# Spacing the activation and split-weight tiles of a two-layer decoder trunk by 64 bytes more than their length

## The chip, the core and the metric

The kernel runs as one program on one core of a Trainium2 chip. The metric is the device time of one execution in microseconds (us). The core has a matrix engine (TensorE: "PE" for its matmuls and "PEld" for its weight loads in the profile), VectorE ("DVE"), ScalarE ("ACT"), GpSimd ("POOL") and a queue engine ("SP") that issues most DMAs. Its working memory has 128 partitions. A tile takes the same range of bytes in each partition that it uses, and "address" below is the first byte of that range within a partition.

## The reference

The reference computes a decoder trunk of two layers on x of 512 tokens by 1024 features, in float32. Cut to the skeleton:

```
hn = rmsnorm(h, norm_mix[layer])
mix = even_mixer(...)  or  odd_mixer(...)      # input projection, attention, output projection
h = h + mix
h = h + square(relu(rmsnorm(h, norm_mlp[layer]) @ w1)) @ w2      # hidden width 4096
out = rmsnorm(h, norm_final)
```

Layer 0 mixes by differential and forgetting attention, layer 1 by a sparse attention that keeps the 128 best keys of each query. What matters here are the products of activations (1024 x 512 tokens) with weight matrices: the input and output projections of both layers and the two MLPs.

## The kernel before

**Split products.** Each of these products is made from two parts per operand. A float32 value is cast to float32r, which gives the high part, and the rest (value minus high part) is the low part. `split` (L178) makes both: ScalarE casts (L179), VectorE or, for some weights, GpSimd subtracts (L180). `gemm_steps` (L351) then adds three matmuls into one PSUM tile for each of the 8 blocks k of 128 input features: high weights times high activations (L355), high weights times low activations (L356), low weights times high activations (L357). Each of them loads 128 x 128 weights and streams 512 token columns of activations past them. The weight load of the next matmul runs while the current matmul streams, so TensorE then reads two things from memory at once: the activations of this matmul and the weights of the next.

**Weights.** `emit_split` (L291) loads 256 columns of a weight matrix into a `raw` tile and splits 128 columns at a time into a `whl` tile of shape (128, 2, 8, 128): 8192 bytes per partition, high parts in the first 4096 bytes and low parts in the last 4096, 512 bytes for each k. There are 3 `whl` buffers, used in turn. `wnext` keeps one tile split ahead of the one in use.

**Activations.** The normed or mixed activations lie in 16 `gh` tiles (8 high, 8 low; `norm` L214, `first_norm` L241, `o_split` L675) of 2048 bytes each. In the MLP (`mlp`, L681) the hidden layer is made in two halves of 2048 features: `proj` (L396) multiplies `gh` with w1, and `fin` (L687) turns each result into a high and a low tile with the tag `act`, 32 tiles of 2048 bytes; `out_gemm` (L629) multiplies the 16 pairs of `act` with w2. The last 128 features of the last product are made in two pieces of 256 columns (`last_pair`, L646).

**Places in memory.** Tiles of a pool lie one behind another, so the address of one moves all that follow it. In the built program `whl` lies at 42560, 50752 and 58944, `gh` at 67136 + 2048 n, and `act` at 134784 + 2048 n in layer 0 and 151168 + 2048 n in layer 1. Modulo 256 this is 64 for all of `whl`, 64 for all of `gh`, and 128 for all of `act`. The slices within a tile begin at multiples of 512 bytes from its start, so every slice has its tile's remainder. The attention's tiles have one remainder per layer: `qk`, `P`, `PT` and `vs` all have 128 in layer 0 and 0 in layer 1. The constant `onesr` has 192, `scr` 64.

**Order.** The order of the work on each engine is the order in which the program is written; `weave` (L364) interleaves the threads of the attention stages by their counts of steps. In the MLPs and output projections TensorE runs the matmuls of `gemm_steps` one after another with nothing between them.

Of the kernel before, what the change touches and what calls it, by code (L numbers as in the profile page):

```python
# [11 lines left out]
F32R = mybir.dt.float32r  # L12
# [5 lines left out]
P = 128  # L18
S = 512
D = 1024  # L20
NT = S // P
KB = D // P
# [16 lines left out]
WHL_BUFS = 3  # L39
# [38 lines left out]
def trunk(ctx, tc, x, norm_mix, w_in_even, b_forget, lambda_q1, lambda_k1, lambda_q2, lambda_k2,  # L78
# [4 lines left out]
    wts = ctx.enter_context(tc.tile_pool(name="wts", bufs=2))  # L83
# [5 lines left out]
    def blk(tag, bufs, shape=(P, S), dt=F32, pool=None):  # L89
        tile_n[0] += 1  # L90
        return (pool or big).tile(list(shape), dt, name=f"{tag}_{tile_n[0]}", tag=tag, bufs=bufs)

    def ptile(tag, bufs):
        tile_n[0] += 1
        return ps.tile([P, S], F32, name=f"{tag}_{tile_n[0]}", tag=tag, bufs=bufs)
# [3 lines left out]
    pT = lambda: ptile("pT", B_PT)  # L99
    pO = lambda: ptile("pO", B_PO)  # L100
    scr = lambda: blk("scr", 5)
    small = lambda n, dt=F32: blk(f"sm{n}", 6, (P, n), dt, sm)


    xv = x.rearrange("o (t p) d -> p (o t) d", p=P)
    load = tc.tile_pool(name="load", bufs=1, reuse_waits="tile")
    lpool = load.__enter__()
    xt = [blk("xw", 4, (P, NT, WC), pool=lpool) for c in range(D // WC)]
    vecs = lpool.tile([16, P], F32, name="vecs")

# [67 lines left out]
    def split(dst_hi, dst_lo, src, eng=None):  # L178
        nc.scalar.copy(dst_hi, src)  # L179
        (eng or nc.vector).tensor_sub(dst_lo, src, dst_hi.bitcast(F32))  # L180
# [33 lines left out]
    def norm(gcol, rope_tab):  # L214
        gh = []
        acc = scr()
        for j in range(KB):
            hi = blk("gh", 16, dt=F32R)
            lo = blk("gh", 16, dt=F32R)
            g = cols[:, gcol + j:gcol + j + 1]  # L220
            nc.scalar.activation(hi, h[j], AF.Copy, scale=g)
            nc.vector.scalar_tensor_tensor(lo, h[j], g, hi.bitcast(F32), op0=OP.mult, op1=OP.subtract)
            gh.append((hi, lo))
            if j == 0:
                nc.scalar.activation(acc, h[j], AF.Square)
            else:
                sq = scr()
                nc.scalar.activation(sq, h[j], AF.Square)
                nc.vector.tensor_add(acc, acc, sq)
        r_tables(rsqrt_cols(acc, 1.0 / D), rope_tab)  # L230
        return gh
# [9 lines left out]
    def first_norm(w, c0):  # L241

        load_x(1)
        emit_split()
        load_x(2)
        load_x(3)
# [44 lines left out]
    def emit_split():  # L291
        w, r0, c0, c, n, wd, lo = plan.pop(0)
        if c == 0:
            raw = blk("raw", RAW_BUFS, (P, KB, WC), F32, wts)
            nc.sync.dma_start(raw[:, :, :wd], w[r0:r0 + D, c0:c0 + wd].rearrange("(k p) c -> p k c", p=P))
            raws[0] = raw
        t = blk("whl", WHL_BUFS, (P, 2, KB, P), F32R, wts)
        split(t[:, 0, :, :n], t[:, 0, :, n:2 * n] if n == 8 else t[:, 1, :, :n], raws[0][:, :, c:c + n], lo)
        ready.append((t, w, r0, c0 + c))

    def wnext(w, r0, c):
        while plan and len(ready) <= AHEAD:
            emit_split()
        t, w_, r_, c_ = ready.pop(0)
        assert (r_, c_) == (r0, c) and w_.tensor.name == w.tensor.name
        return t
# [89 lines left out]
    def proj(w, gh, c0, fin):  # L396
        r = []
        for c in range(0, WC, P):
            wt = wnext(w, 0, c0 + c)
            p = pg()  # L400
            gemm(p, wt, gh)
            fin(p, r.append)
        return r
# [225 lines left out]
    def out_gemm(w, r0, acts, done=None, early=()):  # L629
        nr = len(acts) // KB  # L630
        for s in range(D // WC):
            if done is not None and s == D // WC - 1:
                last_pair(w, r0, acts, s, done)
                return
            pp = early if early and s == 0 else [pg() for c in range(0, WC, P)]
            for r in range(nr):
                for i, p in enumerate(pp):
                    if pp is not early:
                        gemm(p, wnext(w, r0 + r * D, s * WC + i * P), acts[r * KB:(r + 1) * KB], start=(r == 0), stop=(r == nr - 1))
                    if r == nr - 1:  # L640
                        j = s * WC // P + i
                        nc.vector.tensor_add(h[j], h[j], p)  # L642
                        if done is not None:
                            done(j)
# [36 lines left out]
    def mlp(ap, layer, done=None):  # L681
        gh = norm(16 + KB * layer, False)
        half = 2 * D
        w1, w2 = w_mlp_in[layer], w_mlp_out[layer]
        for f0 in range(0, D_FF, half):
            acts = []
            def fin(p, put):  # L687
                t = blk("t", 3, pool=ap)
                nc.vector.scalar_tensor_tensor(t, p, 0.0, r_b, op0=OP.max, op1=OP.mult)  # L689
                hi = blk("act", 32, dt=F32R, pool=ap)  # L690
                lo = blk("act", 32, dt=F32R, pool=ap)
                nc.scalar.activation(hi, t, AF.Square)
                sq = blk("t", 3, pool=ap)
                nc.scalar.activation(sq, t, AF.Square)
                nc.vector.tensor_sub(lo, sq, hi.bitcast(F32))
                put((hi, lo))

            for s in range(half // WC):
                acts += proj(w1, gh, f0 + s * WC, fin)
            out_gemm(w2, f0, acts, done if f0 + half == D_FF else None)  # L700
# [316 lines left out]
```

## Time and profile before

| | |
|---|---|
| median of 3 runs | 1266.65 us (1266.27 to 1266.7) |
| the profiled execution | 1266.42 us, of which 1264.6 us from the first to the last instruction |
| granted TensorE clock | 0.999 |
| matmuls / weight loads | 5882 / 5882 |
| busy: PE / PEld / DVE / ACT / POOL | 99% / 81% / 57% / 44% / 8% |
| HBM read / written | 111.18 MB / 6.29 MB |

Stages by the trace's windows: first norm and first products up to about 60 us, attention of layer 0 to about 230, output projection and MLP of layer 0 to about 620, input products and attention of layer 1 to about 870, output projection and MLP of layer 1 to the end.

A row that groups instructions has the line, the engine, the operation, the tile written and the tiles read (buffer numbers left out), the shapes and the count; behind the first bar the busy time in us and the mean duration of one in ns; behind the second bar the idle time ahead of them, and what ended it. Since matmuls overlap, the duration of one is longer than the distance from its start to the start of the next, and its end is modelled. The distance between starts is called pitch here.

### The profile page before, as it was taken

To read this page: it belongs to the slowest core of one execution; us is meant where nothing else is said; L and a number is where in the kernel's file an instruction comes from. 1 tells how busy PE (TensorE), PEld (TensorE's weight loads), DVE (VectorE), ACT (ScalarE), POOL (GpSimd) and SP (SyncE) were. 2 spreads that over 40 slices of the span, in tenths; PEclk is the share of its full clock that TensorE was granted. 3 is DMA by queue.
4 is the path that set the end of the run, shared out by engine and by line. 5 is a ranking of instruction groups with operands and counts; after the bars stand their busy time and mean duration, and the time that the engine had idled before them with its cause. 6 is when DMAs were issued, how large, how long until landed. Compare 5 with 4: busy or idle time off the path is not lost.

```text
span 1264.6 us, 15517 instructions
## 1 busy us (share of the span) xinstructions
PE 1246.9 (99%) x5882; PEld 1029.2 (81%) x5882; DVE 721.7 (57%) x1386; ACT 558.2 (44%) x1013; POOL 100.0 (8%) x75
## 2 busy tenths in 40 slices
PE   8999999999999999999999999999999999999998
PEld 6778888888888888888788888887888888888887
DVE  7887669664432244434499987787644322444232
ACT  5456667443321133323353578885533211333231
POOL 2000000000000000000114533230000000000000
PEclk9999999999999999999999999999999999999999
DMA  8646342333322233233335344524333223332321
GB/s 240 152 122 165 98 139 79 114 100 100 100 100 98 79 93 98 100 117 109 133 100 153 95 124 117 154 76 133 100 100 98 87 85 97 100 100 100 100 67 67
DMA packets 145898, 138.92 MB, mean 110 GB/s; under 512 B 7480, under 2 KB 130528, under 8 KB 145824
## 3 DMA queue, kind: packets, MB, share of 16 engines
q1 hardware_dynamic: 144848, 136.66, 36.4%
q0 software_dynamic: 528, 0.67, 0.3%
q8 instruction: 46, 0.75, 0.2%
q10 hardware_dynamic: 448, 0.60, 0.2%
q14 instruction: 28, 0.23, 0.1%
HBM read 111.18 MB, written 6.29 MB: 93 GB/s over the span
## 4 chain that ended last, share of the span: by engine, by line
PE 87%; DVE 5%; ACT 3%; DMA 2%; issue 1%; SPq 1%; POOL 0%; POOLq 0%; DVEq 0%; ACTq 0%
PE pg L355 26%; PE pg L357 26%; PE pg L356 26%; DMA raw<-in_w_in_even_dram 2%; PE pT L514 2%; PE pS L480 1%; PE pS L481 1%; ACT P L488 1%; PE pO L533 1%; PE pO L532 1%; DVE whl L180 1%; ACT whl L179 1%; PE pT L449 1%; DVE P L486 1%; DVE PT L180 1%
## 5 line engine op out<-in xcount | busy, mean ns | idle before, releaser
L179 ACT CAST whl<-raw 128x1024 fp32r<-128x1024 f32 (+1 forms) x198 | 206.5, 1044 | 538.6 <-PE pg L357 486.2
L355 PE MATMUL pg<-gh,whl 128*128 128x512 f32 x1064 | 421.3, 397 | 3.9 <-ACT whl L179 3.8
L357 PE MATMUL pg<-gh,whl 128*128 128x512 f32 x1064 | 416.0, 392 | 1.4 <-DVE whl L180 1.3
L356 PE MATMUL pg<-gh,whl 128*128 128x512 f32 x1064 | 415.2, 391 | 0.0
L180 DVE TENSOR_TENSOR whl<-raw,whl 128x1024 fp32r<-128x1024 f32 x174 | 211.4, 1216 | 180.7 <-ACT whl L179 180.4
L357 PEld LDWEIGHTS pg<-gh,whl 128*128 128x128 f32 x1064 | 199.4, 187 | 44.0 <-DVE whl L180 2.5
L355 PEld LDWEIGHTS pg<-gh,whl 128*128 128x128 f32 x1064 | 199.5, 188 | 42.4 <-ACT whl L179 4.9
L356 PEld LDWEIGHTS pg<-gh,whl 128*128 128x128 f32 x1064 | 199.8, 188 | 38.6
L355 PE MATMUL pg<-act,whl 128*128 128x512 f32 (+1 forms) x528 | 204.5, 387 | 0.0
L357 PE MATMUL pg<-act,whl 128*128 128x512 f32 (+1 forms) x528 | 203.4, 385 | 0.0
L356 PE MATMUL pg<-act,whl 128*128 128x512 f32 (+1 forms) x528 | 201.4, 382 | 0.0
L689 DVE SCALAR_TENSOR_TENSOR t<-pg,r_b 128x512 f32<-128x512 f32 x64 | 44.3, 692 | 156.2 <-PE pg L357 153.7
L357 PEld LDWEIGHTS pg<-act,whl 128*128 128x128 f32 x528 | 99.1, 188 | 21.8
L356 PEld LDWEIGHTS pg<-act,whl 128*128 128x128 f32 x528 | 99.1, 188 | 20.9
L355 PEld LDWEIGHTS pg<-act,whl 128*128 128x128 f32 x528 | 99.3, 188 | 18.6
L488 ACT ACTIVATE P<-P,sm 128x128 f32<-128x128 f32 (+3 forms) x128 | 71.7, 561 | 50.2 <-DVE sm L486 49.8
L642 DVE TENSOR_TENSOR h<-h,pg 128x512 f32<-128x512 f32 x46 | 31.4, 687 | 108.3 <-PE pg L357 108.3
L180 POOL TENSOR_TENSOR whl<-raw,whl 128x1024 fp32r<-128x1024 f32 x24 | 57.7, 2406 | 122.2 <-ACT whl L179 100.7
L190 POOL TENSOR_TENSOR sm<-sm,nhalf 128x4 f32<-128x4 f32 (+1 forms) x9 | 10.4, 1153 | 648.1 <-DVE sm L188 648.1
L180 DVE TENSOR_TENSOR PT<-pT,PT 128x384 fp32r<-128x384 f32 (+1 forms) x84 | 49.7, 597 | 19.2 <-ACT PT L179 18.6
L179 ACT CAST PT<-pT 128x384 fp32r<-128x384 f32 (+1 forms) x84 | 42.4, 510 | 13.9 <-PE pT L514 13.3
L514 PE MATMUL pT<-ident,P 128*128 128x128 f32 x280 | 46.5, 275 | 1.7 <-ACT P L501 0.8
(230 smaller groups left out, 1180.6 us busy)
## 6 DMA issues: line engine op xcount, KB each, us to landing
raw<-in_w_mlp_in_dram SPq DMA_DIRECT2D x32, 1024.0 KB, 5.4
raw<-in_w_mlp_out_dram SPq DMA_DIRECT2D x32, 1024.0 KB, 4.8
qk<-qk SPq DMA_DIRECT2D x156, 128.0 KB, 2.3
raw<-in_w_in_even_dram SPq DMA_DIRECT2D x24, 512.0 KB, 4.7
raw<-in_w_in_odd_dram SPq DMA_DIRECT2D x16, 512.0 KB, 4.0
raw<-in_w_in_odd_dram SPq DMA_DIRECT2D x6, 1024.0 KB, 5.1
raw<-in_w_out_even_dram SPq DMA_DIRECT2D x4, 1024.0 KB, 5.2
h<-hd SPq DMA_DIRECT2D x16, 256.0 KB, 5.7
```

The source lines that it names most:

```text
L179: nc.scalar.copy(dst_hi, src)
L180: (eng or nc.vector).tensor_sub(dst_lo, src, dst_hi.bitcast(F32))
L355: nc.tensor.matmul(pout, wt[:, 0, k, :n], a, start=start and k == 0, stop=False)
L356: nc.tensor.matmul(pout, wt[:, 0, k, :n], b, start=False, stop=False)
L357: last_mm[0] = nc.tensor.matmul(pout, wt[:, 1, k, :n], a, start=False, stop=stop and k == KB - 1)
L449: nc.tensor.transpose(q[:, t * P:(t + 1) * P], y[:, t * P:(t + 1) * P], ident)
L480: nc.tensor.matmul(sp[m][:, c], qb[m][:, q], kb[0][m][:, :w], start=True, stop=False)
L481: nc.tensor.matmul(sp[m][:, c], qb[m][:, q], kb[1][m][:, :w], start=False, stop=(rows is None))
L488: nc.scalar.activation(o, o, AF.Exp, bias=st[m][:, t:t + 1], scale=-1.0, accum_out=st[m][:, 4 + t:5 + t])
L514: nc.tensor.transpose(p[:, o - o0 + (t - kt) * P:o - o0 + (t - kt + 1) * P], pt[:, OFF[t] + kt * P:OFF[t] + (kt + 1) * P], ident)
L642: nc.vector.tensor_add(h[j], h[j], p)
L689: nc.vector.scalar_tensor_tensor(t, p, 0.0, r_b, op0=OP.max, op1=OP.mult)
```

## The change

A helper `odd_blk` takes a tile 16 elements (64 bytes) longer than asked and hands out its first n columns. The `whl` tiles and both `act` tiles are made with it:

```diff
+    def odd_blk(tag, bufs, n, dt, pool):
+
+        return blk(tag, bufs, (P, n + 16), dt, pool)[:, :n]
...
-        t = blk("whl", WHL_BUFS, (P, 2, KB, P), F32R, wts)
+        t = odd_blk("whl", WHL_BUFS, 2 * KB * P, F32R, wts).rearrange("p (a k c) -> p a k c", a=2, k=KB)
...
-                hi = blk("act", 32, dt=F32R, pool=ap)
-                lo = blk("act", 32, dt=F32R, pool=ap)
+                hi = odd_blk("act", 32, S, F32R, ap)
+                lo = odd_blk("act", 32, S, F32R, ap)
```

The buffers are then 8256 and 2112 bytes apart. In the built program `whl` lies at 42560, 50816 and 59072, that is 64, 128 and 192 modulo 256. All that follows `whl` moves up by 192 bytes: `gh` to 67328 + 2048 n, remainder 0 for all 16 tiles; `act` to 134976 + 2112 n and 151360 + 2112 n, remainders 64, 128, 192, 0 in turn, so that a high tile and its low tile differ by 64. `qk`, `P`, `PT` and `vs` move together, to 64 in layer 0 and 192 in layer 1; `scr` to 0; `onesr`, `ident` and `raw` stay.

The instructions and their order are the same on every engine, and every shape that an instruction reads or writes. One wait is new, on ScalarE ahead of the first write into `act` in layer 0. Before, the rows there (line, operation, tiles with their numbers, and the semaphores waited for) are:

```order
L179 CAST whl_2810<-raw_2772 128x1024 [waits PE_49,Activation_49]
L179 CAST scr_2728<-scr_2726 128x512 [waits DVE_49,Activation_49]
L236 COPY r_b<-pT_2732 128x512 [waits PE_49]
L692 ACTIVATE act_2766<-t_2764 128x512 [waits DVE_49]
L694 ACTIVATE t_2769<-t_2764 128x512
```

Now, with lines 4 further down in the file, they are:

```order
L183 CAST whl_2810<-raw_2772 128x1024 [waits PE_49,Activation_49]
L183 CAST scr_2728<-scr_2726 128x512 [waits DVE_49,Activation_49]
L240 COPY r_b<-pT_2732 128x512 [waits PE_49]
L696 ACTIVATE act_2766<-t_2764 128x512 [waits DMAHW2_49,DVE_49]
L698 ACTIVATE t_2769<-t_2764 128x512
```

Nothing has moved; the write of the first `act` tile also waits for a DMA (DMAHW2), because the longer tile reaches 64 bytes into the place of a second `qk` tile of the attention before.

## The prediction

> **What bounds the kernel now.** I read the page first, for the engine that sets the time: its span, its busy times and the chain of work that ended last.
>
> ```profile
> span 1264.6 us, 15517 instructions
> PE 1246.9 (99%) x5882; PEld 1029.2 (81%) x5882; DVE 721.7 (57%) x1386; ACT 558.2 (44%) x1013; POOL 100.0 (8%) x75
> PE pg L355 26%; PE pg L357 26%; PE pg L356 26%; DMA raw<-in_w_in_even_dram 2%; PE pT L514 2%; PE pS L480 1%; PE pS L481 1%; ACT P L488 1%; PE pO L533 1%; PE pO L532 1%; DVE whl L180 1%; ACT whl L179 1%; PE pT L449 1%; DVE P L486 1%; DVE PT L180 1%
> ```
>
> TensorE is busy 99% of the span, and the three matmul lines of `gemm_steps` hold 78% of the chain. Next, what TensorE waits for, and what the splits wait for (who waits, for whom, us in total, times, longest):
>
> ```profile
> PE pg L355 <- ACT whl L179: 3.8, 3, 1.6
> PE pg L357 <- DVE whl L180: 1.3, 2, 1.0
> ACT whl L179 <- PE pg L357: 486.2, 137, 6.1
> ```
>
> TensorE waits 5 us in all for weights, while ScalarE waits 486 us for TensorE to free a `whl` buffer. So the time is the number of matmuls by their pitch, and a change reaches it only through the pitch. Is the pitch the same everywhere? The groups by form, over the whole span:
>
> ```profile
> L355 PE MATMUL pg<-gh,whl 128*128 128x512 f32 x1056 | 418.2, 397 | 3.9 <-ACT whl L179 3.8
> L357 PE MATMUL pg<-gh,whl 128*128 128x512 f32 x1056 | 412.8, 392 | 1.4 <-DVE whl L180 1.3
> L356 PE MATMUL pg<-gh,whl 128*128 128x512 f32 x1056 | 412.0, 391 | 0.0
> L355 PE MATMUL pg<-act,whl 128*128 128x512 f32 x496 | 195.4, 394 | 0.0
> L357 PE MATMUL pg<-act,whl 128*128 128x512 f32 x496 | 194.4, 392 | 0.0
> L356 PE MATMUL pg<-act,whl 128*128 128x512 f32 x496 | 192.5, 388 | 0.0
> ```
>
> The change touches these 3168 matmuls on `gh` and 1488 on `act`. The means on `gh` mix the woven attention stages with the unbroken ones, so the same groups from 300 to 420 us, where the MLP of layer 0 runs unbroken, on `gh` first and then on `act`:
>
> ```profile
> L355 PE MATMUL pg<-act,whl 128*128 128x512 f32 x95 | 37.4, 394 | 0.0
> L356 PE MATMUL pg<-act,whl 128*128 128x512 f32 x95 | 36.9, 388 | 0.0
> L357 PE MATMUL pg<-act,whl 128*128 128x512 f32 x94 | 36.9, 392 | 0.0
> L357 PE MATMUL pg<-gh,whl 128*128 128x512 f32 x82 | 31.9, 389 | 0.0
> L355 PE MATMUL pg<-gh,whl 128*128 128x512 f32 x81 | 31.5, 389 | 0.0
> L356 PE MATMUL pg<-gh,whl 128*128 128x512 f32 x81 | 31.5, 389 | 0.0
> ```
>
> On `gh` all three lines have 389 ns, on `act` 394, 388 and 392, a mean of 391.3. Instruction, shape and partner are the same, so 2.3 ns belong to something that `act` has and `gh` hasn't. The stretches confirm it by counting starts instead of modelled ends, 60 us of `gh` alone and 60 us of `act` alone:
>
> ```profile
> 460.00:520.00 60.00, 60.00 (x267) 49.67 (x266) 0.00 (x0) 0.00 (x0) 0.00 (x0) 1.00 0.33 102
> 360.00:420.00 60.00, 60.00 (x264) 49.23 (x263) 0.00 (x0) 0.00 (x0) 1.00 0.27 90
> ```
>
> A count takes in the matmul that began up to 0.39 us ahead, so the pitch is about 60.39/267 = 226.2 and 60.39/264 = 228.8 ns, at a granted clock of 1.00 in both.
>
> **Which difference, and where it starts.** The timeline (start in us, duration) across the step from `gh` to `act`:
>
> ```profile
> 354.46 0.39 PE L355 MATMUL pg<-gh,whl 128*128 128x512 f32 x1
> 354.69 0.39 PE L356 MATMUL pg<-gh,whl 128*128 128x512 f32 x1
> 354.91 0.39 PE L357 MATMUL pg<-gh,whl 128*128 128x512 f32 x1
> 355.14 0.40 PE L355 MATMUL pg<-act,whl 128*128 128x512 f32 x1
> 355.38 0.40 PE L356 MATMUL pg<-act,whl 128*128 128x512 f32 x1
> 355.61 0.39 PE L357 MATMUL pg<-act,whl 128*128 128x512 f32 x1
> 355.84 0.39 PE L355 MATMUL pg<-act,whl 128*128 128x512 f32 x1
> ...
> 357.90 0.39 PE L355 MATMUL pg<-act,whl 128*128 128x512 f32 x1
> ```
>
> From 355.84 to 357.90 are nine pitches: 228.9 ns each. The first three on `act` take 0.70 us, some 0.015 more than three of these. So with the first `act` tile the pace changes at once, passes through a short disturbance and settles. What changed there is the address: `gh` and `whl` both have remainder 64 modulo 256, `act` has 128. Call d the streamed tile's remainder minus that of the weights being loaded, modulo 256: 0 on `gh`, 64 on `act`. My working theory is that the two simultaneous reads disturb each other by d, and that d = 0 is the best of what this trace shows.
>
> **Part by part.**
>
> *`gh` (3168 matmuls).* Afterwards `gh` has 0 and `whl` has 64, 128 or 192, so d is 192, 128 or 64, a third each, and never 0 again. For d = 64 the nearest row is `act`: +2.3 ns. For d = 128 and 192 no unbroken stretch exists. Their lower bound is 0; below zero I see no reason, since 389 ns is the least of all full-width groups but one (388, between 394 and 392). An upper bound for d = 128 is the pair that sums the norm's columns, whose `onesr` weights have 192 while `scr` has 64:
>
> ```profile
> 143.80 0.40 PE L357 MATMUL pg<-gh,whl 128*128 128x512 f32 x1
> 144.03 0.40 PE L208 MATMUL pT<-scr,onesr 128*128 128x512 f32 x1
> 144.27 0.40 PE L209 MATMUL pT<-scr,onesr 128*128 128x512 f32 x1
> 144.51 0.40 PE L355 MATMUL pg<-gh,whl 128*128 128x512 f32 x1
> ```
>
> Its matmuls lie 240 ns apart, 14 above the pitch on `gh`; but these are single steps amid other work, like the disturbance above, and not a settled pace. I take half of the `act` row, 1.2 ns, for each: it is nearer to how `act` settles than to this. Mean (2.3 + 1.2 + 1.2)/3 = 1.6 ns, by 3168 = +5.0 us; ends 0.8 x 3168 = +2.4 (only d = 64 costs) and 2.3 x 3168 = +7.3.
>
> *`act` (1488 matmuls, and 96 of half width that I leave out).* Its remainders go round against three of `whl`, so all four d are equally frequent: mean (0 + 2.3 + 1.2 + 1.2)/4 = 1.2 instead of 2.3, −1.1 x 1488 = −1.7 us. Ends: −2.6 if only d = 64 costs, −0.9 if all but 0 do. As a high tile and its low tile differ by 64, d now changes within each group of three, for which no row stands; it is in the next term.
>
> *Changes of d.* Each new `whl` tile brings a new d. The page has 198 splits into `whl`:
>
> ```profile
> L179 ACT CAST whl<-raw 128x1024 fp32r<-128x1024 f32 (+1 forms) x198 | 206.5, 1044 | 538.6 <-PE pg L357 486.2
> ```
>
> At 0.015 us each, as at 355.14, that is 3.0 us; some go back to a better d, where no such cost need arise, so half: +1.5 us, ends 0 and 3.
>
> *Other engines.* ScalarE and VectorE write the same shapes to other addresses. The subtraction into `PT`, at remainder 128 in layer 0 (first row, 60 to 290 us) and 0 in layer 1 (665 to 890 us), takes the same:
>
> ```profile
> L180 DVE TENSOR_TENSOR PT<-pT,PT 128x384 fp32r<-128x384 f32 x24 | 13.3, 552 | 8.0 <-ACT PT L179 7.9
> L180 DVE TENSOR_TENSOR PT<-pT,PT 128x384 fp32r<-128x384 f32 x32 | 17.6, 553 | 6.7 <-ACT PT L179 6.3
> ```
>
> So 0; and if some got slower, the 486 us that the splits wait for TensorE would cover it. In the attention `qk` with `qk` and `PT` with `vs` keep d = 0.
>
> *The new wait.* It stands ahead of the first write into `act`; queued behind it are the rest of `fin` and the next split. SP issued its last DMA of the attention before 219 us, and the write starts at 278.49:
>
> ```profile
> 218.06 3.67 SPq L668 DMA_DIRECT2D h<-hd  x8
> 278.49 0.63 ACT L692 ACTIVATE act<-t 128x512 fp32r<-128x512 f32 x1 [0.76 <-DVE t L689]
> ```
>
> The DMA has landed some 60 us earlier: 0.
>
> Sum: 5.0 − 1.7 + 1.5 = +4.8 us on the profiled execution's 1266.42 (span 1264.6 and 1.8 around it), 1271.2; the median of the runs lies 0.2 higher, which gives **1271.4 us**. With the ends of the terms, 2.4 − 2.6 + 0 = about 0 to 7.3 − 0.9 + 3 = +9.4, so this case alone spans 1266.5 to 1276.
>
> **The rivals.** A measurement of this kernel can tell about 0.2% (2.5 us) from no change.
>
> *Faster: the streamed tile's own remainder counts, not d.* Then `act` is slow because it stands at 128, and `gh` may be as well off at 0 as at 64. A quarter of `act` stays at 128, and the rest saves 0.75 x 2.3 x 1488 = 2.6 us, or all of it 3.4 if alternating tiles undo the disturbance: 1263.3 to 1264.1. For it: both readings explain the step at 355.14. Against: 0 must be a good remainder too, which no unbroken row shows.
>
> *No change: addresses do not count.* The 2.3 ns could come from something else that sets `act` apart, such as its place far from `whl` or its 32 tiles. Then 1266.6. For it: over the whole span `gh` has means of 397, 391 and 392 ns at one and the same d = 0, so disturbances exist that have nothing to do with remainders. The Trainium skill, in "SBUF — State Buffer", section "Who interferes with whom", gives TensorE two independent read ports, one for the streamed operand and one for weight loads, and says that it never waits on anyone; by that rule this rival holds and the time stays 1266.6 us. The trace agrees only on `gh`, where the pace is even; the 389 against 391.3 ns of otherwise equal matmuls are not explained by it.
>
> *Much slower: d = 128 costs in a settled stream what the pair at 144.03 shows,* 14 ns. The third of `gh` at d = 128 would pay 1056 x 14 = 14.8 us, those at 64 and 192 together 1056 x 3.5 = 3.7, `act` (0 + 2.3 + 14 + 1.2)/4 − 2.3 = +2.1 by 1488 = 3.1, changes 1.5: +23 us, 1289.7. It decides from about 6 ns at d = 128 on. Against: the pair is a single step between other work, and `act` too began above its settled pace.
>
> **How the numbers follow.** The forecast's case has a chance of 0.47, of which 0.09 falls within 2.5 us of no change. No change by addresses has 0.26, faster by the streamed tile's remainder 0.19, much slower 0.08. Faster by over 0.2% is 0.19 (that rival ends at the bound or beyond it), within 0.2% is 0.26 + 0.09 = 0.35, slower 0.38 + 0.08 = 0.46. The range goes from 1263.0, below the faster rival's end, to 1277.0, just above the forecast's upper end; it leaves out the much slower case and little of the rest.
>
> **What would show it.** In the profile after, the groups of L359 to L361 (the old L355 to L357) from 300 to 345 us should show `gh` at 389 to 392 ns, with three levels in turn, one for each `whl` tile (5.44 us of 24 matmuls): the highest at the `whl` tile with remainder 192 (d = 64). `act` should fall from 391.3 towards 390.5. If `gh` stays at 389 with every `whl` tile, d is not the cause and the step "+5.0 on `gh`" is wrong; if `act` stays at 394, 388 and 392, remainders do not count at all. A `gh` level below 389 would make the sign wrong. The wait at the first `act` write should show no idle time beyond 0.76 us.

## The result and the profile after

The changed kernel takes 1282.86 us (median of 4 runs, 1282.12 to 1283.81) against 1266.68 us; the ratio is 1.0127, 95% interval 1.0109 to 1.0145. It is slower, as forecast, but by 16.2 us instead of 4.8, beyond the range. The profiled execution took 1283.07 us.

The page of the changed kernel, the same rows as shown of the kernel before. The old lines 355, 356 and 357 are now 359, 360 and 361.

```profile
span 1281.3 us, 15518 instructions
PE 1263.2 (99%) x5882; PEld 1029.5 (80%) x5882; DVE 722.9 (56%) x1386; ACT 558.0 (44%) x1013; POOL 99.9 (8%) x75
PE pg L359 27%; PE pg L361 27%; PE pg L360 26%; DMA raw<-in_w_in_even_dram 2%; PE pT L518 2%; PE pS L484 1%; PE pS L485 1%; PE pO L537 1%; PE pO L536 1%; ACT P L492 1%; ACT whl L183 1%; DVE whl L184 1%; PE pT L453 1%; PE pT L189 0%; DVE PT L184 0%
```

The span grew by 16.7 us, TensorE's busy time by 16.3, and nobody else's by more than 1.2. What TensorE waits for is what it was (before 3.8 and 1.3):

```profile
PE pg L359 <- ACT whl L183: 3.6, 2, 2.3
PE pg L361 <- DVE whl L184: 1.7, 2, 1.4
```

So TensorE has no new wait; the matmuls themselves follow one another more slowly. The groups by form over the whole span:

```profile
L359 PE MATMUL pg<-gh,whl 128*128 128x512 f32 x1056 | 422.7, 401 | 3.7 <-ACT whl L183 3.6
L361 PE MATMUL pg<-gh,whl 128*128 128x512 f32 x1056 | 417.3, 396 | 1.7 <-DVE whl L184 1.7
L360 PE MATMUL pg<-gh,whl 128*128 128x512 f32 x1056 | 417.1, 395 | 0.0
L361 PE MATMUL pg<-act,whl 128*128 128x512 f32 x496 | 195.1, 393 | 0.0
L359 PE MATMUL pg<-act,whl 128*128 128x512 f32 x496 | 194.8, 393 | 0.0
L360 PE MATMUL pg<-act,whl 128*128 128x512 f32 x496 | 194.4, 392 | 0.0
```

On `gh` 397, 391 and 392 ns became 401, 395 and 396; on `act` the uneven 394, 388 and 392 became 393, 392 and 393. The unbroken stretches show it without the woven stages: `gh` from 300 to 345 us (389 ns in all three lines before) and `act` from 370 to 420.

```profile
L360 PE MATMUL pg<-gh,whl 128*128 128x512 f32 x65 | 25.7, 395 | 0.0
L359 PE MATMUL pg<-gh,whl 128*128 128x512 f32 x65 | 25.7, 395 | 0.0
L361 PE MATMUL pg<-gh,whl 128*128 128x512 f32 x65 | 25.7, 395 | 0.0
...
L359 PE MATMUL pg<-act,whl 128*128 128x512 f32 x73 | 28.7, 394 | 0.0
L361 PE MATMUL pg<-act,whl 128*128 128x512 f32 x73 | 28.6, 392 | 0.0
L360 PE MATMUL pg<-act,whl 128*128 128x512 f32 x72 | 28.2, 392 | 0.0
```

The counts of starts, `gh` from 460 to 520 us and `act` from 365 to 425:

```profile
460.00:520.00 60.00, 60.00 (x260) 48.52 (x259) 0.00 (x0) 0.00 (x0) 0.00 (x0) 1.00 0.30 95
365.00:425.00 60.00, 60.00 (x262) 48.77 (x261) 0.00 (x0) 0.00 (x0) 1.00 0.27 90
```

There were 267 and 264. A pitch of about 60.39/260 = 232.3 ns on `gh` is 6 ns more than before, at the same granted clock of 1.00, and 60.39/262 = 230.5 on `act` is 1.7 more. The time thus went where the forecast looked for it. Adding up the distances from each matmul's start to the next in the two traces gives the split: +13.5 us on full-width `gh` matmuls, +2.8 on `act` and +0.4 on all else, 16.7 together.

### The profile page after: what moved, and what is told of

Same layout as the page of the kernel before. It is cut to its first block, busy times and chain, and to the rows that moved or that the text cites. A ratio compares the mean times of both kernels' runs of the same rounds, so it can differ in the third digit from the quotient of the medians.

```text
span 1281.3 us, 15518 instructions
## 1 busy us (share of the span) xinstructions
PE 1263.2 (99%) x5882; PEld 1029.5 (80%) x5882; DVE 722.9 (56%) x1386; ACT 558.0 (44%) x1013; POOL 99.9 (8%) x75
## 4 chain that ended last, share of the span: by engine, by line
PE 89%; DVE 4%; DMA 3%; ACT 2%; issue 1%; SPq 1%; POOL 0%; POOLq 0%; DVEq 0%; ACTq 0%
PE pg L359 27%; PE pg L361 27%; PE pg L360 26%; DMA raw<-in_w_in_even_dram 2%; PE pT L518 2%; PE pS L484 1%; PE pS L485 1%; PE pO L537 1%; PE pO L536 1%; ACT P L492 1%; ACT whl L183 1%; DVE whl L184 1%; PE pT L453 1%; PE pT L189 0%; DVE PT L184 0%
## 5 line engine op out<-in xcount | busy, mean ns | idle before, releaser
L183 ACT CAST whl<-raw 128x1024 fp32r<-128x1024 f32 (+1 forms) x198 | 206.0, 1042 | 554.9 <-PE pg L361 500.2
L359 PE MATMUL pg<-gh,whl 128*128 128x512 f32 x1064 | 425.8, 401 | 3.7 <-ACT whl L183 3.6
L361 PE MATMUL pg<-gh,whl 128*128 128x512 f32 x1064 | 420.5, 396 | 1.7 <-DVE whl L184 1.7
L360 PE MATMUL pg<-gh,whl 128*128 128x512 f32 x1064 | 420.3, 395 | 0.0
L184 DVE TENSOR_TENSOR whl<-raw,whl 128x1024 fp32r<-128x1024 f32 x174 | 211.4, 1216 | 181.7 <-ACT whl L183 181.3
L194 POOL TENSOR_TENSOR sm<-sm,nhalf 128x4 f32<-128x4 f32 (+1 forms) x9 | 10.4, 1152 | 657.5 <-DVE sm L192 657.5
L183 ACT CAST PT<-pT 128x384 fp32r<-128x384 f32 (+1 forms) x84 | 42.4, 510 | 13.9 <-PE pT L518 13.1
```

Source lines behind the costliest of these rows:

```text
L359: nc.tensor.matmul(pout, wt[:, 0, k, :n], a, start=start and k == 0, stop=False)
L360: nc.tensor.matmul(pout, wt[:, 0, k, :n], b, start=False, stop=False)
L361: last_mm[0] = nc.tensor.matmul(pout, wt[:, 1, k, :n], a, start=False, stop=stop and k == KB - 1)
```

## The experiments

The theory: the pace of the matmuls depends on d, the remainder modulo 256 of the streamed tile's address minus that of the weights being loaded meanwhile, and d = 0 is best. The rivals: the streamed tile's own remainder counts; going round as such counts (that the remainder changes from buffer to buffer, whatever d is); addresses do not count. All kernels below are the kernel before with the edit shown, and compute the whole reference. Where no spacing is said, `whl` has remainder 64. `before` is always the kernel before on the same chip.

### Each half of the change alone

```diff
-        t = blk("whl", WHL_BUFS, (P, 2, KB, P), F32R, wts)
+        t = blk("whl", WHL_BUFS, (P, 2 * KB * P + 16), F32R, wts)[:, :2 * KB * P].rearrange("p (a k c) -> p a k c", a=2, k=KB)
```

> Only the split-weight tiles are spaced by 64 bytes more; act stays at 2048 bytes apart. gh then lies at remainder 0 against weights at 64, 128, 192 as in the changed kernel, act at 64 for all tiles. Theory d (the streamed tile's remainder minus that of the weights being loaded counts, 0 is best): gh pays as in the changed kernel, about 4.8 ns of pitch on 3168 matmuls = 15 us, act has d = 0, 192, 128 in turn and pays some 1 ns more than before on 1488 = 1 to 2 us: 1281 to 1284 us. Rival, going round of act is what costs (high and low tile of one group differ by 64): at most half of the 16 us stay, 1267 to 1275 us.

Measured: 1283.67 us against 1266.47, ratio 1.0134 (1.0120 to 1.0147). All of the loss is there, and the time is in the theory's range. The stretch from 460 to 520 us on `gh`:

```profile
460.00:520.00 60.00, 60.00 (x259) 48.36 (x258) 0.00 (x0) 0.00 (x0) 0.00 (x0) 1.00 0.31 96
```

That is the changed kernel's count to one. Added up, `gh` costs +14.4 us and `act` +3.3, more than the 1 to 2 us expected of it.

```diff
-                hi = blk("act", 32, dt=F32R, pool=ap)
-                lo = blk("act", 32, dt=F32R, pool=ap)
+                hi = blk("act", 32, (P, S + 16), F32R, ap)[:, :S]
+                lo = blk("act", 32, (P, S + 16), F32R, ap)[:, :S]
```

> Only act is spaced by 64 bytes more; weights at 64 and gh at 64 as before, act at 128, 192, 0, 64 in turn. Theory d: gh unchanged at 227 ns, act passes through all four d and has a mean pitch near 230 instead of 228.9: +1 to +3 us, 1267.5 to 1269.5 us. Rival, going round of act is what costs: +8 us or more, over 1274 us.

Measured: 1269.83 us against 1266.47, ratio 1.0023 (1.0014 to 1.0033), just above the theory's range. The groups from 365 to 415 us:

```profile
L357 PE MATMUL pg<-act,whl 128*128 128x512 f32 x73 | 28.8, 395 | 0.0
L355 PE MATMUL pg<-act,whl 128*128 128x512 f32 x73 | 28.7, 393 | 0.0
L356 PE MATMUL pg<-act,whl 128*128 128x512 f32 x72 | 28.3, 392 | 0.0
```

`gh` is as before and `act` costs +3.3 us. A quarter of the `act` matmuls has d = 0 here, yet by the starts they take a mean of 231.2 ns, as those at the other three d (231.0 to 231.3). When d changes within a group of three, a matmul does not show the pace of its own d. The sum, though, is nearly what the paces of the single d add up to: held for whole stretches below, they are 226.7, 228.9, 233.3 and 233.3 ns, a mean of 230.6.

### All tiles at d = 0, in two places

```diff
     def mlp(ap, layer, done=None):
+        ap.tile([P, 48], F32, name=f"gap_{layer}")
         gh = norm(16 + KB * layer, False)
```

> No spacing; a gap of 192 bytes ahead of t and act in both MLPs puts act at remainder 64, as gh and the weights: d = 0 for all. Theory d: act settles at 226.7 ns like gh, 2.25 ns less on 1488 matmuls = -3.3 us: 1263.3 us. Rival, something else sets act apart (its number of tiles, its place high in the partition): 1266.6 us, act stays at durations of 394, 388 and 392 ns.

Measured: 1263.48 us against 1266.47, ratio 0.9976 (0.9967 to 0.9986): 3.0 us faster than the kernel before. `act` from 365 to 415 us:

```profile
L357 PE MATMUL pg<-act,whl 128*128 128x512 f32 x74 | 28.8, 389 | 0.0
L355 PE MATMUL pg<-act,whl 128*128 128x512 f32 x74 | 28.8, 389 | 0.0
L356 PE MATMUL pg<-act,whl 128*128 128x512 f32 x74 | 28.8, 389 | 0.0
```

The 394, 388 and 392 ns are gone and `act` runs like `gh`. The number of tiles is the same and they lie only 192 bytes further up, so it was the remainder.

The second kernel has the same gap and 64 bytes more at the end of the constants, `const.tile([P, 16], F32, name="gap0")`, so that all four kinds of tiles move to 128.

> As the one with all tiles at remainder 64, but with a gap of 64 bytes ahead of raw and the weights: raw, weights, gh and act all at remainder 128. Theory d: only the difference counts, so again 226.7 ns everywhere and 1263.3 us. Rival, the streamed tile's own remainder counts (64 is good, 128 costs 2.3 ns): gh and act both at 391.3 ns of mean duration, +7.3 us from gh and nothing gained on act, 1274 us.

Measured: 1263.64 us against 1266.47, ratio 0.9979 (0.9969 to 0.9988). `gh` from 460 to 520 us and `act` from 365 to 415:

```profile
460.00:520.00 60.00, 60.00 (x266) 49.70 (x265) 0.00 (x0) 0.00 (x0) 0.00 (x0) 1.00 0.34 106
365.00:415.00 50.00, 50.00 (x222) 41.40 (x222) 0.00 (x0) 0.00 (x0) 1.00 0.30 103
```

50.39/222 = 227.0 ns at remainder 128 for both reads. The streamed tile's own remainder, 128, which cost 2.3 ns against weights at 64, is free against weights at 128. The rival that would have made the change faster falls; the difference is what counts.

### `gh` held at one d

```diff
+    gap = ctx.enter_context(tc.tile_pool(name="gap", bufs=1))
+    gap.tile([P, 16], F32, name="gap")
     big = ctx.enter_context(tc.tile_pool(name="big", bufs=1))
...
+        ap.tile([P, 32], F32, name=f"gap_{layer}")
         gh = norm(16 + KB * layer, False)
```

The 16 elements are d = 64; 32 and 48 are 128 and 192. The second gap, 32, 16 or none, keeps `act` at d = 0.

> No spacing; a gap of 64 bytes between the weights and gh puts gh at 128 against weights at 64: d = 64 for gh throughout, act at 64 with d = 0. Theory d with the pitches of the changed kernel (231.7 at d = 64): 3168 x 4 = +13 us on 1263.3: 1276 us. If the pitch that act showed before at the same remainders (128 against 64, 228.9) holds for gh: 3168 x 2.3 = +7 us, 1270.5 us. Rival, it is the change of remainder from one weight tile to the next that costs: 1263 to 1266 us.

> The same with a gap of 128 bytes: gh at 192 against weights at 64, d = 128, act d = 0. Theory d with the changed kernel's 232.6 at d = 128: 3168 x 4.9 = +15.5 us on 1263.3, 1279 us. Rival, change from tile to tile: 1263 to 1266 us.

> The same with a gap of 192 bytes: gh at 0 against weights at 64, d = 192, act at 64 with d = 0. Theory d with the changed kernel's 233.4 at d = 192: 3168 x 5.7 = +18 us on 1263.3, 1281 us. Rival, change from tile to tile: 1263 to 1266 us.

Measured against 1266.53: 1268.31 us, ratio 1.0012 (1.0001 to 1.0023), at d = 64; 1276.59, 1.0078 (1.0049 to 1.0108), at 128; 1278.09, 1.0090 (1.0061 to 1.0119), at 192. The stretch on `gh` from 460 to 520 us, of the three kernels in turn:

```profile
460.00:520.00 60.00, 60.00 (x264) 49.23 (x263) 0.00 (x0) 0.00 (x0) 0.00 (x0) 1.00 0.31 96
```

```profile
460.00:520.00 60.00, 60.00 (x259) 48.27 (x258) 0.00 (x0) 0.00 (x0) 0.00 (x0) 1.00 0.29 88
```

```profile
460.00:520.00 60.00, 60.00 (x259) 48.06 (x258) 0.00 (x0) 0.00 (x0) 0.00 (x0) 1.00 0.29 88
```

264 is the count that `act` had before at the same d = 64 (there from 360 to 420 us); 259 gives 60.39/259 = 233.2 ns. No tile's difference changes here, so going round is not needed for the loss, and that rival falls. The theory's times were 2 to 8 us too high: at d = 64 the settled pitch is the 228.9 ns that `act` showed, not the 231.7 taken from the changed kernel, and not every matmul pays the settled price. Over the whole span `gh` pays +3.8, +13.1 and +14.4 us, or 1.2, 4.1 and 4.5 ns on each of 3168 matmuls. Matched one by one with the kernel before, those in the unbroken stretches of the MLPs pay 2.2, 6.2 and 6.7 ns, the rest, where the mean distance was 237.8 ns before the change already, 0.5, 2.7 and 3.1.

### Is 256 the right modulus?

```diff
-        t = blk("whl", WHL_BUFS, (P, 2, KB, P), F32R, wts)
+        t = blk("whl", WHL_BUFS, (P, 2 * KB * P + 64), F32R, wts)[:, :2 * KB * P].rearrange("p (a k c) -> p a k c", a=2, k=KB)
```

> The weight tiles are spaced by 256 bytes more than their length, act as before. All remainders modulo 256 are those of the kernel before (64, 64, 128), but modulo 512 the weights go round. If the remainder modulo 256 is what counts: 1266.6 us and 389 ns on gh. If a larger one (512 or 1024) counts: gh pays on the tiles that differ, over 1270 us.

Measured: 1266.69 us against 1266.53, ratio 0.9995 (0.9984 to 1.0006). `act` from 360 to 420 us has the very durations of before:

```profile
L355 PE MATMUL pg<-act,whl 128*128 128x512 f32 x88 | 34.7, 394 | 0.0
L357 PE MATMUL pg<-act,whl 128*128 128x512 f32 x88 | 34.5, 392 | 0.0
L356 PE MATMUL pg<-act,whl 128*128 128x512 f32 x88 | 34.1, 388 | 0.0
```

A shift of 256 bytes between the reads changes nothing, so a modulus of 512 or more is out; one of 128 is out by d = 128, which differs from d = 0.

### Why d = 64 was dear in the changed kernel

A third of what `gh` pays at each of the three held d is (3.8 + 13.1 + 14.4)/3 = 10.4 us; the changed kernel pays 13.5, which is 3.1 more. Matched one by one with the kernel before, its matmuls at d = 64 cost 3.2 us, 2.9 ns each, where held throughout they cost 1.2 ns; those at 128 cost 4.6 us and those at 192 cost 5.9. The timeline of the changed kernel shows d = 64 twice: the first matmul on two `whl` tiles at remainder 192, and the first of the tile after each, 24 matmuls later.

```profile
309.27 0.40 PE L359 MATMUL pg<-gh,whl 128*128 128x512 f32 x1
...
314.87 0.39 PE L359 MATMUL pg<-gh,whl 128*128 128x512 f32 x1
```

```profile
889.72 0.39 PE L359 MATMUL pg<-gh,whl 128*128 128x512 f32 x1
...
895.22 0.39 PE L359 MATMUL pg<-gh,whl 128*128 128x512 f32 x1
```

5.60/24 = 233.3 ns in one and 5.50/24 = 229.2 in the other, at the same d. Of the 20 such tiles in the unbroken stretches of the MLPs, 15 run at the higher pace and 5 at the lower (229.0 to 229.7). Two runs ask whether it is the pair of remainders (0 against 192) or what went before. The first holds this pair: gaps of 128 bytes after the constants, 64 ahead of `gh`, 128 ahead of `act`.

> The pair of remainders of the changed kernel's third at d = 64, gh at 0 and weights at 192, but held for every tile; act at 192, d = 0. Theory history (the pace at d = 64 depends on the pace that the tile before left; held throughout it is 228.9 to 229.4 ns as with gh at 128 and weights at 64): 1268.3 us. Rival, the remainders themselves count (0 against 192 costs the 231.7 ns that the changed kernel shows): 3168 x 4 = +13 us on 1263.5: 1276 us.

Measured: 1270.27 us against 1268.64 (this chip was slower with both), ratio 1.0018 (1.0007 to 1.0029). `gh` from 460 to 520 us:

```profile
460.00:520.00 60.00, 60.00 (x264) 49.20 (x262) 0.00 (x0) 0.00 (x0) 0.00 (x0) 1.00 0.29 88
```

In this stretch the pair settles as d = 64 did with 128 and 64. Over the whole span `gh` pays +6.0 us, against +3.8 there, mostly because the MLP of layer 0 runs at the higher pace up to its first step to `act`. From 300 to 345 us this kernel has the first of these rows, and the one with `gh` at 128 and weights at 64 the second:

```profile
300.00:345.00 45.00, 45.00 (x195) 36.44 (x194) 0.00 (x0) 0.00 (x0) 0.00 (x0) 1.00 0.31 95
300.00:345.00 45.00, 45.00 (x199) 36.90 (x198) 0.00 (x0) 0.00 (x0) 0.00 (x0) 1.00 0.33 104
```

By the starts that is 233.3 against 228.9 ns, and the higher pace lasts for 14 weight tiles in a row. So a stream at d = 64 has two paces, at one and the same pair of remainders, and the pair alone does not settle which. The second spaces the weights by 48 elements instead of 16.

> Weight tiles spaced by 192 bytes more instead of 64: they go round as 64, 0, 192, and gh at 128 sees d = 64, 128, 192 in turn, the order of the spacing by 64 alone reversed (there 192, 128, 64); act at 192 sees 128, 192, 0. Theory d with history: d = 128 and 192 at 232.6 to 233.4 ns as ever; d = 64 now follows 192, whose even 233.3 ns it kept in places, so it stays near 233 ns more often: 1283 to 1286 us. Rival, d = 64 is dear because it follows 128: it falls to 229 ns, 1279 to 1281 us.

Measured: 1281.29 us against 1268.64, ratio 1.0106 (1.0058 to 1.0155), which on 1266.6 is 1280.0, the rival's time. `gh` costs +10.0 us, and all 19 tiles at d = 64 in the unbroken stretches of the MLPs run at the lower pace (229.4 to 229.6 ns), like this one in layer 0:

```profile
302.07 0.40 PE L355 MATMUL pg<-gh,whl 128*128 128x512 f32 x1
...
307.58 0.39 PE L355 MATMUL pg<-gh,whl 128*128 128x512 f32 x1
```

5.51/24 = 229.6 ns. But the expectation had the order wrong. The built programs take the three buffers of `whl` in the order first, third, second address, so the weights come as 64, 192, 0 here and as 64, 192, 128 in the changed kernel, and `gh` sees d = 64, 192, 128 in turn here and 192, 64, 128 there. The trace agrees: `act`, at 192 here, runs at 226.6 ns, its d = 0, on every third weight tile, and the first of these comes right behind a `gh` tile at the pace of d = 64, whose weights are at 64. So in the changed kernel d = 64 follows 192 and is dear in most places, and here it follows 128 and is cheap in all 19. That fits the idea that d = 64 can keep the pace of a d = 192 before it, and goes against the rival that it is dear because it follows 128, though the rival's time came out.

It does not prove the idea. `gh` and the weights have the remainders 128 and 64 here, a pair that was at the lower pace when held too; the higher pace was seen only with the pair 0 and 192. Whether the tile before or the pair decides is open, since no run puts the pair 128 and 64 behind d = 192.

### Differences between the steps of 64

The gap ahead of `gh` is 32, 224, 96 or 160 bytes, which is its d, and `act` is read from inside longer tiles, at d = 16, 240, 48 or 208, so that one run holds two differences:

```diff
+                hi = blk("act", 32, (P, S + 64), F32R, ap)[:, 4:S + 4]
+                lo = blk("act", 32, (P, S + 64), F32R, ap)[:, 4:S + 4]
```

The 4 is 60, 12 and 52 in the other three.

> How fine is the remainder? Weights at 64; gh at 96 (d = 32) and act at 80 (d = 16: its tiles are 2304 bytes apart and used from 16 bytes on). If 64-byte steps are what counts and d below 64 acts as 0: gh at 389 ns in the unbroken stretches, act at 389, 1263.5 us. If every offset costs in proportion to d = 64: gh about +0.8 ns on 3168, act +0.4 on 1488: 1266.5 us.

> Offsets below 256: weights at 64, gh at 32 (d = 224), act at 48 (d = 240, tiles 2304 bytes apart and used from 240 bytes on). If remainders count in steps of 64 bytes from the weights' place, d = 192 to 255 is one step: gh and act settle near 233.3 ns like d = 192, 1278.1 + 1484 x 6.6 ns = 1288 us. If only the distance from 0 counts, d = 224 costs as d = 32, within 3 us of 1263.5.

> Two differences not held yet, against weights at 64: gh at 160 (d = 96) and act at 112 (d = 48, tiles 2304 bytes apart and used from 48 bytes on). If the pace falls evenly from 233.3 ns at d = 32 to 228.9 at 64 and 226.7 at 96 and on to a rise before 128: act near 231 ns, gh near 227 to 229, 1266 to 1271 us. Rival, d = 64 is a lone dip between high levels: act and gh both near 233 ns, 1284 us.

> gh at 224 (d = 160) and act at 16 (d = 208, tiles 2304 bytes apart and used from 208 bytes on). If all between 128 and 224 is one high level at 233.3 ns: gh +14 us and act +6.6 ns x 1488 = +9.8 us on 1263.5, 1287 us. Rival, the level differs every few bytes: any value from 1263 to 1287.

Measured: 1285.75 us against 1268.64, ratio 1.0142 (1.0112 to 1.0171); 1282.57 against 1268.64, 1.0116 (1.0051 to 1.0182); 1286.46 against 1265.06 (one run each); 1292.63 against 1265.06 (one run each). The counts, of the four kernels in turn, first `gh` from 460 to 520 us and then `act` from 365 to 415 (the kernel before has 267 and 220):

```profile
460.00:520.00 60.00, 60.00 (x259) 48.19 (x258) 0.00 (x0) 0.00 (x0) 0.00 (x0) 1.00 0.33 100
365.00:415.00 50.00, 50.00 (x218) 40.57 (x217) 0.00 (x0) 0.00 (x0) 1.00 0.28 91
```

```profile
460.00:520.00 60.00, 60.00 (x258) 48.28 (x258) 0.00 (x0) 0.00 (x0) 0.00 (x0) 1.00 0.31 94
365.00:415.00 50.00, 50.00 (x222) 41.42 (x221) 0.00 (x0) 0.00 (x0) 1.00 0.27 91
```

```profile
460.00:520.00 60.00, 60.00 (x259) 48.26 (x258) 0.00 (x0) 0.00 (x0) 0.00 (x0) 1.00 0.34 105
365.00:415.00 50.00, 50.00 (x219) 40.81 (x218) 0.69 (x1) 0.00 (x0) 1.00 0.25 85
```

```profile
460.00:520.00 60.00, 60.00 (x258) 48.24 (x257) 0.00 (x0) 0.00 (x0) 0.00 (x0) 1.00 0.34 105
365.00:415.00 50.00, 50.00 (x215) 40.17 (x214) 0.00 (x0) 0.00 (x0) 1.00 0.25 85
```

The mean distance of the starts in these same two stretches, of these kernels and of those above that hold a d, is the settled pitch (at d = 64 the lower of the two paces):

| d | 0 | 16 | 32 | 48 | 64 | 96 | 128 | 160 | 192 | 208 | 224 | 240 |
|---|---|---|---|---|---|---|---|---|---|---|---|---|
| pitch, ns | 226.7 | 231.7 | 233.3 | 230.0 | 228.9 | 233.3 | 233.3 | 234.3 | 233.3 | 234.7 | 233.3 | 226.7 |

Most of these expectations missed. d = 16 is not as free as 0, d = 224 is not as cheap as the distance of 32 bytes suggests, d = 240 is free and 208 is the dearest. It is one high level near 233 ns with a dip around 48 to 64 and a low place at 240 and 0; the runs do not show how far that place reaches between 208 and 240 or from 0 to 16. The values at 16, 48, 208 and 240 come from `act`, whose tiles then lie 2304 bytes apart.

## Why the prediction was wrong

**The bound: right.** TensorE stays at 99%, no wait of it was added, and the whole change is in the pitch.

**The variable: right.** With weights at 64 a streamed tile at 128 costs, with weights at 128 it does not, and a shift by 256 does nothing. d = 0 is the best of the d held, though 240 equals it, and nothing went below 226.7 ns, so "below zero I see no reason" holds.

**The `gh` term: this is the step that failed.** It said "I take half of the `act` row, 1.2 ns, for each" of d = 128 and 192. Held alone they cost 4.1 and 4.5 ns over the whole span, 6.2 and 6.7 in the unbroken stretches. The forecast's bound for d = 128, 14 ns from a single pair, and its choice, 1.2 ns, lie on both sides; the choice rested on the belief that an unseen d lies near the one seen. The one seen, d = 64, is the dip. With 4.1 and 4.5 in place of 1.2, and 2.3 for d = 64 as forecast, the term would have been (2.3 + 4.1 + 4.5)/3 x 3168 = 11.5 us instead of 5.0; measured are 13.5.

**The d = 64 part of it: right when held, too low when it alternates.** Held, it settles 2.2 ns above d = 0. In the changed kernel most tiles at d = 64 run at the higher pace, 233.3 ns and not 228.9, and over the span they pay 2.9 ns where held ones pay 1.2.

**The `act` term: wrong sign, by the same step.** Forecast −1.7 us, as a mean over four d; measured +2.8, and +3.3 with `act` alone spaced. With the settled paces the same mean is (226.7 + 228.9 + 233.3 + 233.3)/4 = 230.55 ns, 1.65 above the 228.9 of before, and by 1488 that is +2.5 us. The sum was sound and the price of 128 and 192 was not. What d changing within a group of three adds on top is small, 0.3 us in the changed kernel and 0.8 with `act` alone spaced.

**Changes of d: too low, and not a fixed price.** Forecast +1.5 us; what the prices of the held d leave unexplained is 3.1 us on `gh` and 0.3 on `act`. It is not 0.015 us at each new tile: at d = 64 a higher pace lasts over whole tiles. This was not what took the time out of the range: the prices of the held d alone, 10.4 us on `gh` and 2.5 on `act`, give 1279.6 us, beyond 1277.0.

**The signs.** `gh` came out at 395 ns, above the 389 to 392 that was named. The forecast looked for the highest level on the weight tile at d = 64; where the levels differ clearly, it has the lowest: 229.2 ns at 889.72, and 5.57/24 = 232.1 for the tile behind it, at d = 128, up to 900.79.

**Other engines and the new wait: right.** The splits into `whl` take 1042 and 1216 ns (1044 and 1216 before). The first write into `act`, with its new wait, again follows its input by 0.76 us:

```profile
280.86 0.63 ACT L696 ACTIVATE act<-t 128x512 fp32r<-128x512 f32 x1 [0.76 <-DVE t L693]
```

**The rivals.** "No change" falls with the first pair of runs, and with it what the Trainium skill, in "SBUF — State Buffer", section "Who interferes with whom", would make of this case: that TensorE's two read ports are independent and it never waits on anyone. Here the pace of the same matmuls goes from 226.7 to 234.7 ns with nothing changed but the places of tiles in memory; the measurement decides. That the two reads collide in some part of the memory is the obvious reading, but only argued: the runs show that their difference counts, not where they meet. "Much slower", at 1289.7 us, had the right mechanism for d = 128 and too high a price; it stood outside the range, at a chance of 0.08, and the time of 1282.9 us fell between it and the forecast.

## What to carry to other kernels

When streamed activations and weight loads run at once, give all their tiles the same remainder modulo 256: 192 bytes of gap ahead of `act` made this kernel 3.0 us faster (0.9976, 0.9967 to 0.9986), and going round made it 16 us slower. The sign in this trace was that equal matmuls had 389 ns in one stage and 394, 388 and 392 in another: the faster stage tells which difference to copy. An even pace alone tells nothing, for the changed kernel has 395 ns in all three lines on `gh`. One measured difference says little about another: a single value may be the dip of a curve, so a cost for values not seen needs the whole span of what has been seen as its range.

## What was not expected of the hardware

The pace of back-to-back matmuls of 512 columns is a settled pattern that depends on d in steps finer than 64 bytes (226.7 ns at 0, 231.7 at 16, 233.3 at 32, 228.9 at 64), and it is not symmetric (226.7 at 240, 231.7 at 16). At d = 64 it has two paces: the same stream, with `gh` at 0 and weights at 192, ran at 233.3 ns over 14 weight tiles in a row in one stage and at 228.9 in others, and what picks one is open. And when d changes from matmul to matmul, those at d = 0 do not keep their 226.7 ns (231.2 with `act` alone spaced), while the sum stays within 0.6 ns a matmul of the mean of the four paces.
